# A two-layer diffusion backbone on one core: the second layer's decay masks taken from DRAM, and the sums between the layers put first

## The chip, the cores and the metric

The kernel runs on one core of one Trainium2 chip. The metric is the device time of one execution in microseconds (us). Five engines run their own instruction streams: TensorE (PE in the rows; PEld is its weight load), VectorE (DVE), ScalarE (ACT), GpSimd (POOL) and SyncE (SP), which here only issues DMAs.

## The reference

Two layers over 256 latent and 256 context tokens of width 1024. Each layer mixes tokens by three branches, then runs a mixture of 64 experts:

```
z = h @ w_in[l]                          # split into retention q,k,v,g; attention q,k,v; conv; gates
log_gamma = log_sigmoid(decay_logit)     # (2 directions, 8 heads)
scores = (q @ k^T) * decay_in            # decay_in[i,j] = exp(log_gamma * (i - j)) for i >= j, else 0
y_inner = scores @ v                     # within a chunk of 128 tokens; a state carries to the next chunk
branches = retention, attention (16 heads, 4 kv heads), depthwise conv (width 31) + LayerNorm + silu
mix = (sum_b sigmoid(gate_b) * (branch_b @ w_b)) @ w_out
x = LayerNorm(alpha * x + mod * mix)
f = routed experts (top 8 of 64) + shared expert
x = LayerNorm(alpha * x + mod * f)       # what layer 1 starts from
```

`decay_in` depends on `decay_logit` and positions alone, not on the tokens, so the masks of layer 1 can be worked out at any time after the log of the decay is known.

## The kernel before

**Weights.** fp32 products are made of parts: a weight slab is loaded (tile `raw`, 1 MB per DMA on the SP queue), ScalarE copies it rounded to `whi` (L90), and VectorE or GpSimd subtracts to get the low part `wlo` (L91). `mm` (L228) then does three matmuls per tile (hi·hi, lo·hi, hi·lo). `split_on_pool(n)` gives every n-th piece's low part to GpSimd; 0 means none.

**Start.** Tokens are transposed and modulated into `hb` (hi and lo), the first slab of `w_in` (S_RQ, the retention queries) is split, and TensorE begins with S_RQ. At the same place a series of 25 small VectorE operations (L330 to L352) works out the log of the decays (`lg`, `lgx`) from `decay_logit`.

**Retention** (L606 on). For each of 8 heads `decays` (L613 to L629) builds two mask tiles of 128x512: `ml` (VectorE L618 and L619, GpSimd add L620, ScalarE Exp L621, VectorE adds the identity, L624 twice) and `mx` (ScalarE Exp L626 and L627, GpSimd add L628). The score tile `sa` (L682) is the product of a transposed PSUM tile and `ml`; it is split into `sah` and `sal` for the next matmul. The depthwise convolution (tiles `cacc`, L571, 31 taps by VectorE) has a low priority and fills the stretches where VectorE has nothing else; its `G` (L564) comes from the projections S_CU.

**Merges.** `merge(0)` and `merge(2)` follow: four steps each, in which gate projections give `sg` (ScalarE), an output slab `w_o` is loaded and multiplied, and a part of the modulation matrix (`w_ada`) of later use is worked through. In layer 0 they also end the convolution: the last `cy` goes into `csum` (GpSimd L585), which TensorE multiplies with a mean matrix (L579).

**Between the layers** (L1737 to L1784, written out by hand under `manual_schedule`). Each token tile t of 4 has a base (L1728, L1729) and 8 rows per token from the experts, loaded as four `yb` tiles of 1 MB out of a pool of 7 buffers. `summed(t)` adds rows 0 to 3 on TensorE (identity matmuls L1737, into PSUM) and rows 4 to 7 on VectorE (L1738, L1740), then both (L1743), the gate (L1744) and the residual (L1745), and the statistics. `normal(t)` (L1783, L1784) normalizes `x` on ScalarE; `enter_mix` transposes it (TensorE L382), modulates it and splits it into `hb`. Then layer 1's S_RQ begins. The order of the loop is normal(t), enter_mix(t), summed(t+1).

**Order.** Outside `manual_schedule` a scheduler puts the instructions of each engine in order, by priorities and estimated readiness; the listings below show what it made of each kernel. Tiles of tag `act` (L363, `actt`) share 3 buffers, among them `sg` of the gates and the mask's helper `m`.

Of the kernel before, what the change touches and what calls it, by code (L numbers as in the profile page):

```python
# [21 lines left out]
T = 256  # L22
L = 2
# [46 lines left out]
def body(ctx, tc, A, out):  # L70
# [80 lines left out]
    sp.dma_start(cv, A["cond"].rearrange("p (k n) -> p k n", k=8))  # L151
    FIRST = (0, 4, 1, 5, 2, 6, 3, 7)
# [93 lines left out]
    act.activation(cv, cv, AF.Silu)  # L246
    modrow = dr.tile([L, 6, 2, D], F32, name="modrow")
# [81 lines left out]

    lg = consts.tile([128, L * 16], F32, name="lg")  # L330
    sp.dma_start(lg, A["decay"].to_broadcast([128, L * 16]))
    e_, s_, s2, t_ = (consts.tile([128, L * 16], F32, name=n) for n in ("e_", "s_", "s2", "t_"))
    act.activation(t_, lg, AF.Abs)
    act.activation(e_, t_, AF.Exp, scale=-1.0)
    dve.tensor_scalar(s_, e_, 2.0, None, op0=OP.add)
    dve.reciprocal(s_, s_)
    dve.tensor_tensor(s_, s_, e_, op=OP.mult)
    dve.tensor_tensor(s2, s_, s_, op=OP.mult)
    dve.memset(t_, 1.0 / 19)
    for n in (17, 15, 13, 11, 9, 7, 5, 3, 1):  # L340
        dve.tensor_tensor(t_, t_, s2, op=OP.mult)
        dve.tensor_scalar(t_, t_, 1.0 / n, None, op0=OP.add)
    dve.tensor_tensor(t_, t_, s_, op=OP.mult)
    dve.tensor_scalar(lg, lg, 0.0, None, op0=OP.min)
    dve.scalar_tensor_tensor(lg, t_, -2.0, lg, op0=OP.mult, op1=OP.add)

    lgx = consts.tile([128, 3, L * 8], F32, name="lgx")
    lg4 = lg.rearrange("p (l w h) -> p l w h", l=L, w=2)
    lgo = lgx.rearrange("p i (l h) -> p i l h", l=L)
    dve.tensor_scalar(lgo[:, 0], lg4[:, :, 1], -1.0, None, op0=OP.mult)  # L350
    dve.tensor_scalar(lgo[:, 1], lg4[:, :, 0], 256.0, None, op0=OP.mult)
    dve.tensor_scalar(lgo[:, 2], lg4[:, :, 1], 256.0, None, op0=OP.mult)  # L352

# [6 lines left out]
    x1d = dr.tile([512, D], F32, name="x1d")  # L360

# [13 lines left out]
    def enter(x, w, mod, hi, lo, halves=(0, 1)):  # L375
# [12 lines left out]

    def enter_mix(x, t, mod, halves=(0, 1)):
        ts = slice(t * 128, t * 128 + 128)  # L390
        enter(x, t // 2, mod, hb[:, 0:8, ts], hb[:, 8:16, ts], halves)
# [26 lines left out]
    def mix(l):  # L418
# [30 lines left out]
        with pool_of(f"mix{l}") as M:  # L449
# [18 lines left out]
            def merge(br, bT, between=None):  # L468
# [32 lines left out]
            with pool_of(f"conv{l}") as PC:  # L501
                conv_tile, conv_norm, conv_out = conv(l, PC, NQ, NS, lambda t: projT(wi(S_CU + t), NQ), newT)
                with pool_of(f"ret{l}") as P, split_on_pool(SHARE["ret"][l]):
                    bT = newT()
                    for p in retention(l, P, NQ, NS, NT, lambda s, nt: proj(wi(s), hT, nt),
                                       lambda s: projT(wi(s), NQ), bT):
                        conv_tile(2 * p)
                        conv_tile(2 * p + 1)
                with weight_pool(f"w_merge{l}", *((2, 3), (0, 0))[l]), split_on_pool(3):
                    merge(0, bT, conv_norm)  # L510
                    merge(2, conv_out(newT()))
# [94 lines left out]
    def retention(l, P, NQ, NS, NT, proj_r, proj_t, bT):  # L606
        delta = P.tile([128, 2, T], F32, name="delta")
        sp.dma_start(delta.rearrange("p j i -> p (j i)"), A["delta"])

        def two(name, dt=F32):  # L610
            return P.tile([128, 2, T], dt, name=name, tag=name, bufs=2)

        def decays(head):  # L613

            gf, gb = lg[:, l * 16 + head:l * 16 + head + 1], lg[:, l * 16 + 8 + head:l * 16 + 9 + head]
            ng, f256, b256 = (lgx[:, i, l * 8 + head:l * 8 + head + 1] for i in range(3))
            ml, mx, m2 = two("ml"), two("mx"), actt("m2").rearrange("p (j i) -> p j i", j=2)
            dve.tensor_scalar(ml, delta, 0.0, gf, op0=OP.max, op1=OP.mult)  # L618
            dve.tensor_scalar(m2, delta, 0.0, ng, op0=OP.min, op1=OP.mult)  # L619
            pool.tensor_tensor(ml, ml, m2, op=OP.add)  # L620
            act.activation(ml, ml, AF.Exp)  # L621
            for j in range(2):
                sl = ml[:, j, j * 128:j * 128 + 128]
                dve.tensor_tensor(sl, sl, ident, op=OP.add)  # L624
            m2 = actt("m2").rearrange("p (j i) -> p j i", j=2)
            act.activation(mx, delta, AF.Exp, bias=f256, scale=gf)  # L626
            act.activation(m2, delta, AF.Exp, bias=b256, scale=ng)  # L627
            pool.tensor_tensor(mx, mx, m2, op=OP.add)  # L628
            return ml, mx  # L629

        masks = {0: decays(0)}
        for half in range(2):
# [15 lines left out]
            for pr in range(2):  # L648
# [16 lines left out]
                for hh in range(2):  # L665
                    head = half * 4 + pr * 2 + hh
                    ml, mx = masks.pop(head)
                    if head < 7:
                        masks[head + 1] = decays(head + 1)
# [338 lines left out]
    def moe(l, merged, x_src):  # L1008
# [6 lines left out]
        with pool_of(f"moe{l}") as K, ExitStack() as es:  # L1015
# [698 lines left out]
            with pool_of(f"post{l}") as P:  # L1714
# [16 lines left out]
                def summed(t):  # L1731

                    y = yb[t]
                    o = [bank() for _ in range(2)]
                    for i in range(4):
                        for c in range(2):
                            pe.matmul(o[c], ident, y[i // 2][:, i % 2, c * 512:c * 512 + 512], start=i == 0, stop=i == 3)  # L1737
                    dve.tensor_tensor(y[2], y[2], y[3], op=OP.add)  # L1738
# [17 lines left out]
                with tc.manual_schedule():  # L1756
# [61 lines left out]
    last_modulation()  # L1818
    for k in range(8):
# [101 lines left out]
```

## Time and profile before

| | us |
|---|---|
| median of 3 runs (lowest, highest) | 2847.43 (2845.09, 2849.63) |
| the profiled execution | 2846.9 |
| its span in the trace | 2845.1 |
| TensorE busy | 2573.5 (90%) |
| VectorE, ScalarE, GpSimd busy | 1658.2, 1313.1, 670.9 |

TensorE is the engine that sets the end nearly everywhere: a gain is a stretch in which it now waits and would not. The span splits into the start (to 52 us), layer 0's mixers (to 840), its experts (to 1583), the passage between the layers (to 1690), layer 1's mixers (to 2290) and its experts and end. A row of a timeline gives the start, the busy time, engine, line, operation, out<-in, the count, and in brackets the idle time before it with what released it.

### The profile page before, as it was taken

How to read it: one execution, taken by the hardware profiler on the slowest of the kernel's cores; microseconds unless marked ns; L12 is line 12 of the kernel's file. 1: busy time of each engine (PE TensorE's matmuls, PEld its weight loads, DVE VectorE, ACT ScalarE, POOL GpSimd, SP SyncE). 2: the span in 40 equal slices, each digit the busy share in tenths (PEclk: the TensorE clock that was granted, in tenths of full speed). 3: DMA queues.
4: the chain of work that ended last, by engine and by line, in shares of the span. 5: the costliest groups of instructions: out<-in, count | busy, mean ns of one | idle time of the engine just before them, and what ended most of it. 6: DMA issues, size and time to landing. Idle time of an engine off the chain costs nothing. (4 is left out here: it accounts for less than half of the span.)

```text
span 2845.1 us, 39754 instructions
## 1 busy us (share of the span) xinstructions
PE 2573.5 (90%) x14811; PEld 1865.2 (66%) x14811; DVE 1658.2 (58%) x2967; ACT 1313.1 (46%) x2392; POOL 670.9 (24%) x447
## 2 busy tenths in 40 slices
PE   6999999999987899999999588888989799999995
PEld 4878777788777655555555268877978655554542
DVE  4588795258847555555554577887587722231223
ACT  3443425247742355555555346445477333343431
POOL 2444311222233211122221045532312300000000
PEclk8999999999998899999999798888999799999998
DMA  5212256621152499999999842235415399999996
GB/s 218 75 61 73 85 199 235 223 104 38 64 203 94 192 365 402 405 396 395 399 394 382 347 151 89 90 119 183 174 66 182 122 387 423 421 372 395 417 412 269
DMA packets 118903, 684.13 MB, mean 240 GB/s; under 512 B 21936, under 2 KB 24624, under 8 KB 45744
## 3 DMA queue, kind: packets, MB, share of 16 engines
q1 hardware_dynamic: 92544, 624.80, 56.1%
q0 software_dynamic: 20496, 41.98, 3.9%
q10 hardware_dynamic: 5664, 14.75, 1.3%
q8 instruction: 119, 1.95, 0.3%
q14 instruction: 80, 0.66, 0.1%
HBM read 651.76 MB, written 61.93 MB: 251 GB/s over the span
## 5 line engine op out<-in xcount | busy, mean ns | idle before, releaser
L90 ACT ACTIVATE whi<-raw 128x1024 fp32r<-128x1024 f32 x444 | 457.7, 1053 | 263.4 <-PE mm L228 147.9
L91 POOL TENSOR_TENSOR wlo<-raw,whi 128x1024 fp32r<-128x1024 f32 x140 | 345.7, 2479 | 721.4 <-ACT whi L90 653.8
L91 DVE TENSOR_TENSOR wlo<-raw,whi 128x1024 fp32r<-128x1024 f32 x304 | 374.9, 1254 | 195.9 <-ACT whi L90 191.5
L228 PE MATMUL mm<-whi,hb 128*128 128x256 f32 (+1 forms) x2080 | 423.2, 300 | 29.5 <-ACT whi L90 7.9
L228 PE MATMUL mm<-hb,whi 128*128 128x512 f32 (+1 forms) x1536 | 404.4, 351 | 11.2 <-ACT whi L90 6.2
L228 PEld LDWEIGHTS mm<-whi,hb 128*128 128x128 f32 x2080 | 346.0, 200 | 39.9 <-issue 11.8
L1543 PE MATMUL mm<-raw,xw 128*64 128x512 f32 x1408 | 331.2, 600 | 0.0
L1613 POOL DMA_INDIRECT y<-y,ix x94 | 95.9, 1021 | 976.1 <-ACT y L1609 934.3
L228 PE MATMUL mm<-wlo,hb 128*128 128x256 f32 (+1 forms) x1040 | 310.1, 299 | 12.1 <-POOL wlo L91 8.7
L228 PEld LDWEIGHTS mm<-hb,whi 128*128 128x128 f32 x1536 | 271.2, 196 | 48.2 <-ACT whi L90 6.8
L571 DVE SCALAR_TENSOR_TENSOR cacc<-G,cpk,cacc 128x512 f32<-128x512 f32 (+1 forms) x464 | 287.6, 620 | 10.3
L228 PE MATMUL mm<-hb,wlo 128*128 128x512 f32 (+1 forms) x768 | 269.5, 352 | 4.5 <-POOL wlo L91 3.8
L228 PE MATMUL mm<-whi,xp 128*128 128x512 f32 x736 | 263.3, 411 | 1.7 <-ACT whi L90 1.7
L228 PEld LDWEIGHTS mm<-wlo,hb 128*128 128x128 f32 x1040 | 207.8, 200 | 16.7 <-POOL wlo L91 9.7
L1543 PEld LDWEIGHTS mm<-raw,xw 128*64 128x64 f32 x1408 | 94.6, 136 | 162.4 <-issue 156.7
L228 PE MATMUL mm<-bT,whi 128*128 128x512 f32 (+1 forms) x768 | 193.3, 342 | 0.5 <-ACT sg L459 0.2
L1105 DVE SCALAR_TENSOR_TENSOR hidp<-mm,tab,sgl 128x256 f32<-128x256 f32 x86 | 41.6, 483 | 234.4 <-ACT sgl L1101 233.5
L228 PEld LDWEIGHTS mm<-whi,xp 128*128 128x128 f32 x736 | 139.9, 190 | 50.8 <-ACT whi L90 9.4
L91 DVE TENSOR_TENSOR xp<-tr,xp 128x512 fp32r<-128x512 f32 (+2 forms) x126 | 59.6, 492 | 194.2 <-ACT xp L90 156.2
L1609 ACT ACTIVATE y<-mm 128x512 f32<-128x512 f32 (+1 forms) x188 | 110.1, 594 | 130.2 <-PE mm L1600 69.2
L228 PE MATMUL mm<-wlo,xp 128*128 128x512 f32 x400 | 161.1, 403 | 7.3 <-DVE wlo L91 7.1
L228 PEld LDWEIGHTS mm<-hb,wlo 128*128 128x128 f32 x768 | 150.1, 196 | 25.3 <-POOL wlo L91 4.7
(657 smaller groups left out, 4352.9 us busy)
## 6 DMA issues: line engine op xcount, KB each, us to landing
raw<-in_w_exp SPq DMA_DIRECT2D x384, 1024.0 KB
raw<-in_w_in SPq DMA_DIRECT2D x76, 1024.0 KB
raw<-in_w_ada SPq DMA_DIRECT2D x48, 1024.0 KB
raw<-in_w_o SPq DMA_DIRECT2D x32, 1024.0 KB
yb<-y SPq DMA_DIRECT2D x24, 1024.0 KB
mod<-modrow SPq DMA_DIRECT2D x12, 512.0 KB
raw<-in_w_shared SPq DMA_DIRECT2D x6, 1024.0 KB
x1d<-xr ACTq DMA_DIRECT2D x6, 512.0 KB
```

The source lines that it names most:

```text
L90: act.activation(hi, src, AF.Copy)
L91: eng.tensor_tensor(lo, src, hi, op=OP.subtract)
L228: pe.matmul(o, l_, r_, start=start and i == 0, stop=stop and i == len(ops) - 1)
L571: dve.scalar_tensor_tensor(v(y if j == 30 else acc), G[:, :, j:j + T], cpk[:, t, j:j + 1], v(acc), op0=OP.mult, op1=OP.add)
L1105: dve.scalar_tensor_tensor(o[:n], b[:n, 256:512], gate[:n], sg[:n], op0=OP.mult, op1=OP.mult)
L1543: pe.matmul(os_[s][0][half], xhs[s][0](k)[:, half], raws[index[r, i // 2]][:, k % 4 * 512:k % 4 * 512 + 512], start=k == 0, stop=k == 7)
L1609: act.activation(ys[b][:n, c * 512:c * 512 + 512], o[c], AF.Copy)
L1613: pool.indirect_dma_start(out=y8s[s, b][:], in_=ys[b][:n], in_offset=None, out_offset=bass.IndirectOffsetOnAxis(ap=tabs[s][b][1][:n, 1:2], ...
```

## The change

1. `lg` is loaded second of all and the decay series stands at the head of the program. The first S_RQ slab has its low parts on VectorE.
2. `decays` becomes a function of the whole program. In layer 0's merges `decays_ahead` makes the masks of layer 1's 8 heads, one head at each of the 8 steps, with a priority offset of -100, and stores `ml` and `mx` in DRAM (256 KB each). Layer 1's retention loads them (3 buffers each).
3. Between the layers `summed` is divided into `half` (the TensorE part) and the rest. half(0) and half(1) stand first, half(t+2) behind the entry of tile t; summed(t+1) comes ahead of the low parts of tile t's `hb`, and normal(t+1) behind them. S_RQ's low parts of layer 1 go to GpSimd.

```diff
+    lg = consts.tile([128, L * 16], F32, name="lg")
+    sp.dma_start(lg, A["decay"].to_broadcast([128, L * 16]))
     FIRST = (0, 4, 1, 5, 2, 6, 3, 7)
...
+    def decays_ahead(P, head):
+        ml, mx = (P.tile([128, 2, T], F32, name=n, tag=n, bufs=1) for n in ("ml", "mx"))
+        delta = actt("delta").rearrange("p (j i) -> p j i", j=2)
+        flat = lambda z: z.rearrange("p j i -> p (j i)")
+        sp.dma_start(flat(delta), A["delta"])
+        decays(1, head, delta, ml, mx)
+        for z, m in enumerate((ml, mx)):
+            sp.dma_start(decayed[head, z], flat(m))
...
-            hilo(hi[:, 4 * c:4 * c + 4], lo[:, 4 * c:4 * c + 4], h_.rearrange("p (k n) -> p k n", k=4))
+            if lows is None:
+                hilo(hi_, lo_, h_)
+            else:
+                act.activation(hi_, h_, AF.Copy)
+                lows.append(partial(dve.tensor_tensor, lo_, h_, hi_, op=OP.subtract))
...
+                    if each:
+                        with tc.high_priority(offset=-100):
+                            each(s)
...
-                    merge(0, bT, conv_norm)
-                    merge(2, conv_out(newT()))
+                    ahead = [None, None]
+                    if l == 0:
+                        W = ds_.enter_context(pool_of("decays"))
+                        ahead = [lambda s: decays_ahead(W, s), lambda s: decays_ahead(W, 4 + s)]
+                    merge(0, bT, conv_norm, ahead[0])
+                    merge(2, conv_out(newT()), None, ahead[1])
...
+        def weights_of(head):
+            ml, mx = (two(n, bufs=2 + l) for n in ("ml", "mx"))
+            if l == 0:
+                decays(l, head, delta, ml, mx)
+            else:
+                for z, m in enumerate((ml, mx)):
+                    sp.dma_start(m.rearrange("p j i -> p (j i)"), decayed[head, z])
             return ml, mx
...
-                        ready[l + 1, S_RQ] = [piece(w, j, 4) for j in range(2)]
+                        with split_on_pool(1):
+                            ready[l + 1, S_RQ] = [piece(w, j, 4) for j in range(2)]
+                    half(0)
+                    half(1)
                     summed(0)
...
+                        normal(0)
                         for t in range(NT):
-                            normal(t)
-                            enter_mix(xs[t], t, mod)
+                            lows = []
+                            enter_mix(xs[t], t, mod, lows)
+                            if t + 2 < NT:
+                                half(t + 2)
                             if t + 1 < NT:
                                 summed(t + 1)
+                            for low_ in lows:
+                                low_()
+                            if t + 1 < NT:
+                                normal(t + 1)
...
+    with split_on_pool(0):
+        ready[0, S_RQ] = slab(A["w_in"][S_RQ])
```

VectorE at the start, before; `t__130` is the series, `ml` and `m_409` the first head's masks.

```order
L343 TENSOR_TENSOR t__130<-t__130,s__128 128x32
L345 SCALAR_TENSOR_TENSOR lg<-t__130,lg 128x32
L350 TENSOR_SCALAR lgx<-lg 128x16
L351 TENSOR_SCALAR lgx<-lg 128x16
L352 TENSOR_SCALAR lgx<-lg 128x16
L618 TENSOR_SCALAR ml<-delta,lg 128x512
L619 TENSOR_SCALAR m_409<-delta,lgx 128x512
L618 TENSOR_SCALAR ml<-delta,lg 128x512
L624 TENSOR_TENSOR ml<-ml,cst 128x128 x2
```

VectorE at the same place, after; `h__374` is the last piece of the modulated tokens.

```order
L1880 TENSOR_SCALAR h__368<-xT,modT 128x256 x2
L1880 TENSOR_SCALAR h__374<-xT,modT 128x256 x2
L1881 TENSOR_TENSOR hb<-h__368,hb 128x512
L1881 TENSOR_TENSOR hb<-h__374,hb 128x512
L92 TENSOR_TENSOR wlo<-raw,whi 128x1024 x2
L372 TENSOR_SCALAR ml<-delta,lg 128x512
L373 TENSOR_SCALAR m_420<-delta,lgx 128x512
L372 TENSOR_SCALAR ml<-delta,lg 128x512
```

The series has gone from this place, and the two low parts of S_RQ stand directly behind the last `hb`.

VectorE between the layers, before, from the end of tile 0's sum to the start of tile 1's; `x_15181` is tile 0, `h__15283` and `h__15295` are its two modulated halves, `mm_15306` is TensorE's sum of tile 1.

```order
L1745 TENSOR_TENSOR x_15181<-x_15181,yb 128x1024
L525 BN_STATS bst<-x_15181 128x6 x2
L526 BN_AGGR mv<-bst 128x2
L1783 SCALAR_TENSOR_TENSOR nm<-mv,ny 128x1
L91 TENSOR_TENSOR hb<-h__15283,hb 128x4x128
L91 TENSOR_TENSOR hb<-h__15295,hb 128x4x128
L1738 TENSOR_TENSOR yb<-yb 128x2048
L1740 TENSOR_TENSOR yb<-yb 128x1024
L1743 TENSOR_TENSOR yb<-yb,mm_15306 128x512
```

VectorE at the same place, after; `x_15322` is tile 0, `x_15323` tile 1, `h__15434` and `h__15445` are tile 0's modulated halves.

```order
L570 BN_STATS bst<-x_15322 128x6 x2
L571 BN_AGGR mv<-bst 128x2
L1829 SCALAR_TENSOR_TENSOR nm<-mv,ny 128x1
L1781 TENSOR_TENSOR yb<-yb 128x2048
L1783 TENSOR_TENSOR yb<-yb 128x1024
L1786 TENSOR_TENSOR yb<-yb,mm_15406 128x512
L1786 TENSOR_TENSOR yb<-yb,mm_15407 128x512
L1787 TENSOR_TENSOR yb<-yb,mod_15340 128x1024
L1788 TENSOR_TENSOR x_15323<-x_15323,yb 128x1024
L570 BN_STATS bst<-x_15323 128x6 x2
L571 BN_AGGR mv<-bst 128x2
L1841 TENSOR_TENSOR hb<-h__15434,hb 128x4x128
```

The two low parts of tile 0's `hb` have moved behind the whole of tile 1's sum, which now follows tile 0's `nm` directly. On TensorE, the sum of tile 1 stands ahead of tile 0's transposes and each later sum moves up by one transpose; S_RQ's first matmuls come ahead of tile 2's transposes.

The SP queue in layer 0's merges, before.

```order
L128 DMA raw<-in_w_ada 128x2048 x4
L128 DMA raw<-in_w_o 128x2048
L128 DMA raw<-in_w_in 128x2048
L128 DMA raw<-in_w_ada 128x2048 x4
L128 DMA raw<-in_w_o 128x2048
L128 DMA raw<-in_w_in 128x2048
L128 DMA raw<-in_w_ada 128x2048 x4
L128 DMA raw<-in_w_o 128x2048
```

The SP queue there, after; `decayed` is the DRAM copy of the masks.

```order
L392 DMA decayed<-mx 128x512
L392 DMA decayed<-ml 128x512
L129 DMA raw<-in_w_ada 128x2048
L129 DMA raw<-in_w_in 128x2048
L129 DMA raw<-in_w_ada 128x2048
L389 DMA delta<-in_delta 128x512
L129 DMA raw<-in_w_ada 128x2048 x3
L392 DMA decayed<-ml 128x512
L392 DMA decayed<-mx 128x512
L129 DMA raw<-in_w_o 128x2048
L129 DMA raw<-in_w_ada 128x2048
L129 DMA raw<-in_w_in 128x2048
```

Two stores of a head and one load of `delta` now stand among the weight loads of each step, here one pair directly ahead of a `w_o` load. In layer 1's retention 16 loads of masks stand among the `w_in` loads, and between the layers all 16 `yb` loads now precede the next `w_in` slab, of which one stood ahead of the last `yb` before.

## Rows read from the trace of the kernel before

**Rows 1.** Windows: length, busy PE PEld DVE ACT POOL, clock, DMA share, GB/s

```profile
350.00:600.00 250.00, 249.14 (x1547) 191.51 (x1546) 138.35 (x204) 81.19 (x114) 47.32 (x30) 1.00 0.57 211
1602.00:1617.00 15.00, 6.50 (x14) 2.49 (x12) 14.09 (x15) 0.50 (x2) 0.00 (x0) 0.84 1.02 425
1690.00:1890.00 200.00, 173.50 (x1221) 164.54 (x1221) 159.95 (x293) 110.19 (x153) 106.13 (x63) 0.86 0.26 89
1890.00:1930.00 40.00, 30.85 (x254) 28.05 (x253) 37.10 (x69) 15.68 (x25) 9.66 (x6) 0.87 0.45 166
```

**Rows 2.** Timeline of TensorE at the start: start, busy, work, [idle before <-releaser]

```profile
51.15 0.58 PE L228 MATMUL mm<-wlo,hb 128*128 128x256 f32 x1 [7.18 <-POOL wlo L91]
```

**Rows 3.** Timeline of GpSimd at the start

```profile
38.17 2.88 POOL L91 TENSOR_TENSOR wlo<-raw,whi 128x1024 fp32r<-128x1024 f32 x1 [13.54 <-ACT whi L90]
46.09 1.44 POOL L620 TENSOR_TENSOR ml<-ml,m 128x512 f32<-128x512 f32 x1 [5.04 <-DVE m L619]
...
48.71 4.76 POOL L91 TENSOR_TENSOR wlo<-raw,whi 128x1024 fp32r<-128x1024 f32 x2
```

**Rows 4.** Timeline of VectorE at the start

```profile
38.75 2.35 DVE L341 TENSOR_TENSOR t__130<-t__130,s 128x32 f32<-128x32 f32 x1
```

**Rows 5.** Timeline of TensorE between the layers

```profile
1618.49 1.97 PE L382 MATMUL tr<-cst,x 128*128 128x128 f32 x8 [9.99 <-ACT x L1784]
...
1648.53 0.38 PE L228 MATMUL mm<-whi,hb 128*128 128x256 f32 x1 [1.98 <-DVE yb L1743]
...
1658.85 7.03 PE L1737 MATMUL mm<-yb,cst 128*128 128x512 f32 x16
...
1672.70 0.55 PE L228 MATMUL mm<-whi,hb 128*128 128x256 f32 x1 [3.56 <-DVE yb L1743]
```

**Rows 6.** Timeline of VectorE between the layers

```profile
1605.11 2.35 DVE L91 TENSOR_TENSOR wlo<-raw,whi 128x1024 fp32r<-128x1024 f32 x2
1607.38 2.29 DVE L1738 TENSOR_TENSOR yb<-yb 128x2048 f32<-128x2048 f32 x1
```

**Rows 7.** Timeline of the SP queue between the layers

```profile
1592.10 40.69 SPq L1772 DMA_DIRECT2D yb<-y  x15
```

**Rows 8.** Waits of TensorE, 1690 to 1930 us: total, times, longest

```profile
PE tr L228 <- DVE sa L682: 7.9, 5, 4.6
...
PE mm L228 <- DVE sal L91: 4.4, 2, 3.1
...
PE mm L228 <- DVE G L564: 3.2, 2, 2.6
```

**Rows 9.** Groups on VectorE, 1660 to 1890 us: busy, mean ns, idle before

```profile
L618 DVE TENSOR_SCALAR ml<-delta,lg 128x512 f32<-128x512 f32 x8 | 8.9, 1108 | 0.0
L624 DVE TENSOR_TENSOR ml<-ml,cst 128x128 f32<-128x128 f32 x16 | 8.1, 528 | 3.8 <-ACT ml L621 3.7
...
L619 DVE TENSOR_SCALAR m<-delta,lgx 128x512 f32<-128x512 f32 x8 | 5.7, 714 | 0.0
```

**Rows 10.** Tile ml, 1650 to 1900 us: nanoseconds min/median/max

```profile
L624 DVE TENSOR_TENSOR ml<-ml,cst x16: 277/286/2385, 1689.9 to 1881.1; 128x128 f32<-128x128 f32 x16
L618 DVE TENSOR_SCALAR ml<-delta,lg x8: 475/478/2601, 1686.6 to 1844.3; 128x512 f32<-128x512 f32 x8
```

**Rows 11.** Timeline of all engines, end of layer 0's convolution

```profile
437.74 1.28 POOL L585 TENSOR_TENSOR csum<-csum,cy 128x512 f32<-128x512 f32 x1 [2.39 <-DVE cy L571]
...
442.05 1.02 PE L579 MATMUL aux<-csum,mean_d 128*128 128x512 f32 x2
```

**Rows 12.** Timeline of ScalarE about a table load

```profile
1772.28 0.47 ACT L242 ACTIVATE rs<-aux,eps 128x256 f32<-128x256 f32 x1 [0.79 <-PE aux L692]
1772.78 1.28 ACT L560 ACT_TABLE_LOAD   x1
1774.07 0.38 ACT L560 ACTIVATE sg<-mm 128x256 f32<-128x256 f32 x1
```

**Rows 13.** Timeline of ScalarE in a merge of layer 0

```profile
393.55 2.01 ACT L90 ACTIVATE whi<-raw 128x1024 fp32r<-128x1024 f32 x2 [7.17 <-DMA raw<-in_w_o]
```

More of the change, by code (lines that the diff above doesn't have):

```diff
@@ L1 @@
 import numpy as np
+from functools import partial
 from contextlib import ExitStack, contextmanager
@@ L246, in body @@
     act.activation(cv, cv, AF.Silu)
+    e_, s_, s2, t_ = (consts.tile([128, L * 16], F32, name=n) for n in ("e_", "s_", "s2", "t_"))
+    act.activation(t_, lg, AF.Abs)
+    act.activation(e_, t_, AF.Exp, scale=-1.0)
+    dve.tensor_scalar(s_, e_, 2.0, None, op0=OP.add)
+    dve.reciprocal(s_, s_)
+    dve.tensor_tensor(s_, s_, e_, op=OP.mult)
+    dve.tensor_tensor(s2, s_, s_, op=OP.mult)
+    dve.memset(t_, 1.0 / 19)
+    for n in (17, 15, 13, 11, 9, 7, 5, 3, 1):
+        dve.tensor_tensor(t_, t_, s2, op=OP.mult)
+        dve.tensor_scalar(t_, t_, 1.0 / n, None, op0=OP.add)
+    dve.tensor_tensor(t_, t_, s_, op=OP.mult)
+    dve.tensor_scalar(lg, lg, 0.0, None, op0=OP.min)
+    dve.scalar_tensor_tensor(lg, t_, -2.0, lg, op0=OP.mult, op1=OP.add)
+    lgx = consts.tile([128, 3, L * 8], F32, name="lgx")
+    lg4 = lg.rearrange("p (l w h) -> p l w h", l=L, w=2)
+    lgo = lgx.rearrange("p i (l h) -> p i l h", l=L)
+    dve.tensor_scalar(lgo[:, 0], lg4[:, :, 1], -1.0, None, op0=OP.mult)
+    dve.tensor_scalar(lgo[:, 1], lg4[:, :, 0], 256.0, None, op0=OP.mult)
+    dve.tensor_scalar(lgo[:, 2], lg4[:, :, 1], 256.0, None, op0=OP.mult)
     modrow = dr.tile([L, 6, 2, D], F32, name="modrow")
@@ L327, in mod_b @@
         return t
[L330 to L352, printed above, removed]
     h2d = dr.tile([512, D], F32, name="h2d")
@@ L360, in body, with decays @@
     x1d = dr.tile([512, D], F32, name="x1d")
+    decayed = dr.tile([8, 2, 128, 2 * T], F32, name="decayed")
+    def decays(l, head, delta, ml, mx):
+        gf, gb = lg[:, l * 16 + head:l * 16 + head + 1], lg[:, l * 16 + 8 + head:l * 16 + 9 + head]
+        ng, f256, b256 = (lgx[:, i, l * 8 + head:l * 8 + head + 1] for i in range(3))
+        m2 = actt("m2").rearrange("p (j i) -> p j i", j=2)
+        dve.tensor_scalar(ml, delta, 0.0, gf, op0=OP.max, op1=OP.mult)
+        dve.tensor_scalar(m2, delta, 0.0, ng, op0=OP.min, op1=OP.mult)
+        pool.tensor_tensor(ml, ml, m2, op=OP.add)
+        act.activation(ml, ml, AF.Exp)
+        for j in range(2):
+            sl = ml[:, j, j * 128:j * 128 + 128]
+            dve.tensor_tensor(sl, sl, ident, op=OP.add)
+        m2 = actt("m2").rearrange("p (j i) -> p j i", j=2)
+        act.activation(mx, delta, AF.Exp, bias=f256, scale=gf)
+        act.activation(m2, delta, AF.Exp, bias=b256, scale=ng)
+        pool.tensor_tensor(mx, mx, m2, op=OP.add)
+    def decays_ahead(P, head):
[6 more added lines that the diff above has]
+            sp.dma_start(decayed[head, z], flat(m))
     def actt(name):
@@ L373, in after_norm, with enter @@
         return f[:, 0], f[:, 1]
-    def enter(x, w, mod, hi, lo, halves=(0, 1)):
+    def enter(x, w, mod, hi, lo, halves=(0, 1), lows=None):
         for c in halves:
@@ L386, in enter, with enter_mix @@
                 act.activation(h_[:, ks], p[:, ks], AF.Identity, bias=b, scale=f)
-            hilo(hi[:, 4 * c:4 * c + 4], lo[:, 4 * c:4 * c + 4], h_.rearrange("p (k n) -> p k n", k=4))
-    def enter_mix(x, t, mod, halves=(0, 1)):
+            hi_, lo_, h_ = hi[:, 4 * c:4 * c + 4], lo[:, 4 * c:4 * c + 4], h_.rearrange("p (k n) -> p k n", k=4)
+            if lows is None:
[3 more added lines that the diff above has]
+                lows.append(partial(dve.tensor_tensor, lo_, h_, hi_, op=OP.subtract))
+    def enter_mix(x, t, mod, lows):
         ts = slice(t * 128, t * 128 + 128)
-        enter(x, t // 2, mod, hb[:, 0:8, ts], hb[:, 8:16, ts], halves)
+        enter(x, t // 2, mod, hb[:, 0:8, ts], hb[:, 8:16, ts], lows=lows)
     def row(name):
@@ L466, in keep_gate, with merge @@
                 sp.dma_start(gd[s, :, :NQ], sg)
-            def merge(br, bT, between=None):
+            def merge(br, bT, between=None, each=None):
                 for s in range(4):
+                    if each:
+                        with tc.high_priority(offset=-100):
+                            each(s)
                     if between and s == 3:
@@ L508, in mix @@
                         conv_tile(2 * p + 1)
-                with weight_pool(f"w_merge{l}", *((2, 3), (0, 0))[l]), split_on_pool(3):
-                    merge(0, bT, conv_norm)
-                    merge(2, conv_out(newT()))
+                with weight_pool(f"w_merge{l}", *((2, 3), (0, 0))[l]), split_on_pool(3), ExitStack() as ds_:
+                    ahead = [None, None]
[4 more added lines that the diff above has]
+                    merge(2, conv_out(newT()), None, ahead[1])
             open_aux(2)
@@ L606, in retention, with two @@
     def retention(l, P, NQ, NS, NT, proj_r, proj_t, bT):
[L607 to L628, printed above, removed]
+        def two(name, dt=F32, bufs=2):
+            return P.tile([128, 2, T], dt, name=name, tag=name, bufs=bufs)
+        if l == 0:
+            delta = two("delta", bufs=1)
+            sp.dma_start(delta.rearrange("p j i -> p (j i)"), A["delta"])
+        def weights_of(head):
+            ml, mx = (two(n, bufs=2 + l) for n in ("ml", "mx"))
+            if l == 0:
+                decays(l, head, delta, ml, mx)
+            else:
+                for z, m in enumerate((ml, mx)):
+                    sp.dma_start(m.rearrange("p j i -> p (j i)"), decayed[head, z])
             return ml, mx
-        masks = {0: decays(0)}
+        masks = {0: weights_of(0)}
         for half in range(2):
@@ L668, in retention @@
                     if head < 7:
-                        masks[head + 1] = decays(head + 1)
+                        masks[head + 1] = weights_of(head + 1)
                     o = 64 * hh
@@ L1729, in base, with half @@
                     dve.scalar_tensor_tensor(xs[t], xs[t], ALPHA, f, op0=OP.mult, op1=OP.add)
-                def summed(t):
+                sums = {}
+                def half(t):
                     y = yb[t]
-                    o = [bank() for _ in range(2)]
+                    o = sums[t] = [bank() for _ in range(2)]
                     for i in range(4):
@@ L1737, in summed @@
                             pe.matmul(o[c], ident, y[i // 2][:, i % 2, c * 512:c * 512 + 512], start=i == 0, stop=i == 3)
+                def summed(t):
+                    y, o = yb[t], sums.pop(t)
                     dve.tensor_tensor(y[2], y[2], y[3], op=OP.add)
```

## The prediction

> **What bounds the kernel now.** I read the windows by stage first, to find where TensorE waits, then its waits in those stages, then the timelines around them. Layer 0's merges have no room: TensorE is busy 249.14 of 250 us there. Layer 1's retention has some: 173.50 of 200 us at a granted clock of 0.86, with VectorE busy 159.95, and the stretch behind it has 30.85 of 40 with VectorE at 37.10 [rows 1]. The start has one wait of 7.18 us for GpSimd's low part [rows 2]. Between the layers TensorE waits for `x`, which comes out of VectorE's chain (9.99 us for the first tile), and for the PSUM banks that VectorE frees late [rows 5]. So the change touches three places where TensorE waits and one where it does not.
>
> **A, the start.** GpSimd makes S_RQ's first low part at 38.17 in 2.88 us, then takes up the first head's mask add, which waits 5.04 us for VectorE's `m`; only at 48.71 do the next low parts start [rows 3]. VectorE's `m` is late because of the series of 25 small operations, one of which took 2.35 us beside GpSimd [rows 4]. After the change the series is done while tokens are still loaded, and the two low parts stand on VectorE directly behind `hb`; a pair takes 2.35 us there [rows 6]. The second is then ready near 41.5, before TensorE has finished the first (43.97, which is 51.15 less 7.18) [rows 2]. The wait of 7.2 goes, and the first low part comes about 0.8 us sooner than 38.17 + 2.88 = 41.05. The load of `lg` costs one issue ahead of the `w_ada` loads. I take **-8**, between -6.5 (the low parts stretched by GpSimd's next one, as the 0.2 us operation was) and -8.7. What is late next at the start is S_RK's low part behind the same mask add, but TensorE has the second half of S_RQ to do first.
>
> [...]
>
> **B, layer 1's retention.** Gone from VectorE: 8.9 + 8.1 + 5.7 = 22.7 us [rows 9], from 32 instructions whose undisturbed durations are 0.48 and 0.28 us and whose longest are 2.6 and 2.4 [rows 10]; GpSimd's 16 adds and ScalarE's 24 exponentials go too. Of TensorE's waits those for `sa` (7.9 us) and `sal` (4.4) follow from `ml` or from a VectorE stretched beside GpSimd, 12.3 in all; of the 3.2 for `G` I count half, since the convolution's filling work then ends sooner [rows 8]. That is **-14**. The lower bound on the gain is half of `sa`'s wait, -4, if what follows it is late in its own right; the upper is nearly all of the stretch's idle 26.5 us [rows 1], -24. Added are 16 loads of 256 KB: 4.2 MB at the 425 GB/s seen between the layers is 10 us over a stretch whose DMA share is 0.26 [rows 1], with three buffers for each mask, so they lie beside other work. They stand in SP's queue ahead of `w_in` loads; a load that waits for its buffer holds those back, and the `whi` copies after them. That price I bound by the same -4.
>
> **C, layer 0's merges.** The 22.7 us come back here as 8 heads, but beside a TensorE that is full. What can end later is the convolution. VectorE's new order has the masks of nearly four heads ahead of the last `cy`: 3.75 heads at 2 x 0.48 + 2 x 0.28 = 1.5 us, 5.7 us, and with some stretching [rows 10] about 7.5. GpSimd's `csum` ends at 437.74 + 1.28 = 439.02 and TensorE takes it at 442.05 [rows 11], so 3.0 of it is hidden: **+4.5**. The matmuls queued behind that one (a gate projection) wait with it. From the second merge on VectorE has room. At best 0, if the scheduler's place for the matmul leaves it room; at worst +16: the ScalarE order has 13 more table loads in these merges (7 fewer in layer 1's retention), 13 x 1.28 [rows 12] = 16.6 us, all of it in the way of `sg`.
>
> In this trace the activation ahead of a table load ends right before it and the next one starts right behind its 1.28 us [rows 12]. The Trainium skill ("ScalarE: Activation LUTs", What ACT_TABLE_LOAD costs) gives 1283 ns and a drain of about 1380 ns more, 2.66 us for a switch. By it the worst case would be an estimated 35 us instead of 16.6; no drain is seen in these rows, so it adds nothing to the sum.
>
> **D, between the layers.** Two low parts leave VectorE's chain, 2.35 us ahead of tile 0's first sum [rows 6]; GpSimd has nothing there. In before a tile takes 1618.49 - 1607.38 = 11.1 us from VectorE's first add to TensorE's transposes [rows 5, 6]. Sixteen loads of 1.05 MB from 1592.10 [rows 7] at 425 GB/s [rows 1] end at 1631.6 if buffers never hold them; the 14th, the last that TensorE's sum of tile 3 needs, lands near 1627. In the new order that sum stands ahead of S_RQ. With its 7.03 us [rows 5], a little more at a lower clock, behind tile 1's transposes it ends near 1638, and S_RQ starts there instead of at 1648.53: -10.5. The 7.03 us no longer stand in the middle of S_RQ, and the wait of 3.56 behind them goes: -10.6 more, -21.1 together. Against that stands the entry of tile 3: 1631.6 + 11.1 = 1642.7 for its transposes, and some 4 us for modulation and parts, 1647; S_RQ's first half with tile 2's transposes, 10.3 us as from 1648.53 to 1658.85 [rows 5], is done at 1648.3. That is level, and any slip shows; I allow 3 us for it: **-18**, between -11 (only the earlier start) and -23. One `w_in` load that stood ahead of the last `yb` now stands behind it, but the `yb` stream ends some 11 us sooner.
>
> **E, the last passage.** VectorE's and TensorE's orders are as before there: 0.
>
> **The sum**: -8 - 14 + 4.5 - 18 = -35.5. The profiled execution took 2846.9, which gives 2811.4; the median of the runs shown is 0.5 above it, so I forecast **2812**.
>
> **Rivals.**
> 1. The retention's gain is given back by the convolution. For it: VectorE is busy 37.1 of 40 us behind the retention, TensorE waits there too [rows 1], so VectorE may be the bound with its taps. Against it: those 22.7 us leave just this engine. B is then -3: 2823.
> 2. The merges pay fully, C at +16: 2823 or 2824. For it, TensorE has no idle time there; against it, the gate matmuls and the `w_ada` work lie between `sg` and its use.
> 3. All waits go: B -24, C 0, D -23, A -8: -55, 2792. For it: the clock of 0.86 rises when TensorE waits less. Against it: other waits follow.
> 4. Slower. In SP's order the two stores of a head stand directly ahead of a `w_o` load in the merges. A store waits for GpSimd's add, which waits for the exponentials and for one of three shared buffers that the gates' `sg` also use. The `w_o` load comes just in time already: ScalarE waits 7.17 us for one [rows 13]. The gains of A, B and D are 40 us; this decides from a delay of (40 + 6) / 8 = 5.8 us at each of 8 steps, and at 6.5 us, 52 in all, gives 2859.
> 5. The change does not do what it says: layer 1's mask loads come late and TensorE waits for them as it did for `sa`, and TensorE's sums between the layers wait for buffers as long as before. A alone less C remains: -8 + 4.5, 2844.
>
> **How the numbers follow.** Forecast 0.50, rival 1 0.20, rival 2 0.12, rival 3 0.10, rival 4 0.04, rival 5 0.04. No change means within 0.2%, 5.7 us, what a measurement of this kernel can tell. Faster: 0.50 + 0.20 + 0.12 + 0.10 = 0.92; same 0.04 (rival 5); slower 0.04. The range: 2796, half-way into rival 3, to 2833, past rivals 1 and 2 together with a D of -11. The forecast's own range is 2804 to 2821.
>
> **What would show it.** A: no wait for a GpSimd low part near 44, S_RQ's second low part used at about 43. B: `sa` and `sal` no longer among TensorE's longer waits, no `L618`-like rows in layer 1. C: a wait of TensorE for `csum` of about 4 us near 435, and otherwise a full window. D: S_RQ starting some 46 us after the first `yb` issue instead of 56, with loads running without a gap. Wrong is the forecast if TensorE waits for `w_o` in every merge step, if layer 1's retention keeps some 20 idle us per 200, or if tile 3's entry leaves a wait of 10 us or more.

## The result, and the profile after

The changed kernel takes 2796.09 us in the median (2792.94 to 2800.77), the kernel before beside it 2846.38: a ratio of 0.9823 (95% interval 0.9806 to 0.984), 50 us faster. Forecast were 2812 us, with 2804 to 2821 as the forecast's own range and 2796 to 2833 with its rivals: the direction is right, but the time lies below the first range and on the very edge of the second, and the gain is 1.4 times what was forecast. The profiled execution took 2795.08, its span is 2792.9.

The same instructions in both traces (TensorE's order is nearly the same) give marks, and the time between two marks is what a stretch cost. A lead, below, is by how much a matmul comes sooner than the same one of the other kernel. In us:

| from, to | before | after | difference | forecast |
|---|---|---|---|---|
| start, sum of the convolution (L579, L624) | 442.1 | 434.8 | -7.2 | A -8, C +4.5 |
| that sum, first sum of expert rows (`mm<-yb`) | 1157.1 | 1157.6 | +0.5 | |
| that, first transposes of S_RQ's result (`tr<-cst,z`) | 87.0 | 65.2 | -21.8 | D -18 |
| those, first matmul of layer 1's merge (`mm<-bT`) | 217.6 | 186.4 | -31.2 | B -14 |
| that, transposes of `xr` at layer 1's experts | 314.7 | 321.6 | +6.9 | 0 |
| those, first sum of the last passage (`mm<-yb`) | 591.7 | 592.2 | +0.5 | 0 |

The sum is -52.3, the difference of the spans. The retention alone is 17 us over its forecast, as much as the whole excess (52 for 35.5); the first two rows together are 3 over, the passage 4, and a row that was not in the forecast takes 7 back.

**The start.** TensorE of the changed kernel (the row's columns are as in [rows 2]) uses the first low part at 40.05, and no wait is left until 44 us:

```profile
40.05 0.58 PE L231 MATMUL mm<-wlo,hb 128*128 128x256 f32 x1 [0.46 <-DVE wlo L92]
```

VectorE makes both low parts in 2.36 us behind `hb`; the first mask operation behind them takes 2.61 us beside GpSimd instead of 0.48:

```profile
38.76 2.36 DVE L92 TENSOR_TENSOR wlo<-raw,whi 128x1024 fp32r<-128x1024 f32 x2 [0.26 <-ACT whi L91]
41.04 2.61 DVE L372 TENSOR_SCALAR ml<-delta,lg 128x512 f32<-128x512 f32 x1
```

The matmul that stood at 51.15 [rows 2] now stands at 42.77: -8.4, where -8 was forecast.

**Layer 0's merges.** From the matmuls at 379 us to those at 588 the lead over before falls from 9.4 to 6.0, so the merges cost 3.4. TensorE's waits in the stretch from 350 to 600 us (total, times, longest), in before:

```profile
PE mm L228 <- POOL wlo L91: 0.9, 1, 0.9
```

and after:

```profile
PE mm L231 <- POOL wlo L92: 1.7, 1, 1.7
PE aux L624 <- POOL csum L630: 1.5, 1, 1.5
PE mm L321 <- DVE G L609: 1.1, 1, 1.1
PE mm L231 <- DVE wlo L92: 0.7, 1, 0.7
```

TensorE waits 1.5 for `csum`, not 4.5. The low part of GpSimd's that it waited for in before as well now stands behind a mask add and costs 0.8 more, and a low part of VectorE's costs 0.7 (the wait for `G` comes ahead of the matmuls at 379). ScalarE's new table loads are there, 21 in this stretch against 7 (two of the groups, busy time and mean ns), and none of the waits above is for `sg`:

```profile
L497 ACT ACT_TABLE_LOAD x8 | 10.3, 1283 | 0.8 <-issue 0.6
...
L380 ACT ACT_TABLE_LOAD x7 | 9.0, 1283 | 14.4 <-issue 9.5 <-DMA delta<-in_delta 4.9
```

**Between the layers.** The 16 `yb` loads are issued without a long gap (before: 15 in 40.69 us and the last 10 us later [rows 7]):

```profile
1585.47 32.60 SPq L1815 DMA_DIRECT2D yb<-y  x16
```

TensorE's sums follow each other, and the wait for `x` is 1.48 and 1.95 where it was 9.99 for the first tile [rows 5]:

```profile
1592.44 17.04 PE L1776 MATMUL mm<-yb,cst 128*128 128x512 f32 x32 [16.53 <-DMA yb<-y]
1610.96 1.09 PE L415 MATMUL tr<-cst,x 128*128 128x128 f32 x8 [1.48 <-ACT x L1830]
...
1621.37 1.34 PE L415 MATMUL tr<-cst,x 128*128 128x128 f32 x8 [1.95 <-ACT x L1830]
...
1630.46 0.68 PE L231 MATMUL mm<-whi,hb 128*128 128x256 f32 x1
```

S_RQ starts 45.0 us after the first issue (1630.46 - 1585.47); it was 56.4.

**Layer 1's retention.** The windows of the changed kernel (columns as in [rows 1]): the merges, 15 us between the layers, and the retention between its marks:

```profile
350.00:600.00 250.00, 244.94 (x1553) 188.82 (x1551) 149.99 (x232) 115.50 (x152) 66.06 (x45) 1.00 0.61 223
1605.00:1620.00 15.00, 12.68 (x35) 5.53 (x33) 13.87 (x19) 6.40 (x15) 0.00 (x0) 1.00 1.01 421
1657.70:1844.00 186.30, 178.29 (x1378) 169.34 (x1377) 159.77 (x286) 97.83 (x140) 89.31 (x49) 0.97 0.34 119
```

The retention between the same marks in the kernel before:

```profile
1686.20:1903.80 217.60, 190.41 (x1357) 180.92 (x1356) 176.51 (x323) 122.15 (x170) 111.66 (x65) 0.87 0.25 88
```

TensorE's idle time falls from 27.2 (217.60 - 190.41) to 8.0 us, which is 19.2 of the 31.2. The other 12.1 are busy time: the matmuls take 178.29 instead of 190.41, at a mean granted clock of 0.97 instead of 0.87 (a mean of stretches at 2.4 GHz and stretches at 1.2). What a level costs can be read from two pieces of the retention in before, the first at 1.2 GHz and the second at 2.4:

```profile
1706.00:1716.00 10.00, 8.83 (x34) 7.79 (x34) 4.66 (x7) 5.84 (x9) 5.51 (x3) 0.50 0.13 25
1716.00:1764.00 48.00, 43.87 (x350) 42.11 (x349) 38.16 (x73) 33.24 (x47) 28.25 (x16) 1.00 0.30 106
```

That is 0.26 us of busy time a matmul against 0.13. By the means, some 55 of 217.6 us were at the lower level in before and some 11 of 186.3 after, in one piece near the end:

```profile
1660.00:1816.00 156.00, 148.07 (x1175) 140.91 (x1174) 135.09 (x241) 84.08 (x117) 83.71 (x44) 1.00 0.36 125
1817.00:1826.00 9.00, 9.00 (x36) 7.68 (x36) 6.49 (x13) 3.26 (x6) 2.36 (x1) 0.50 0.33 117
```

What TensorE waited for in the retention of before, beside `sa` (7.9), `sal` (4.4) and `G` (3.2) of [rows 8]:

```profile
PE tr L643 <- DVE z L412: 3.4, 2, 2.1
PE mm L228 <- ACT sah L90: 2.7, 1, 2.7
PE mm L228 <- ACT rg L663: 2.5, 1, 2.5
PE mm L228 <- ACT sg L560: 2.3, 1, 2.3
```

What it waits for there now:

```profile
PE mm L231 <- DVE sal L92: 4.5, 5, 2.2
PE mm L231 <- ACT sah L91: 1.0, 1, 1.0
PE mm L231 <- ACT sg L605: 0.8, 1, 0.8
PE tr L231 <- DVE sa L719: 0.7, 1, 0.7
PE tr L680 <- DVE z L450: 0.5, 1, 0.5
PE mm L231 <- DVE G L609: 0.2, 1, 0.2
```

`sa` is all but gone, and so are `G`, `z` and `rg`; `sal`, which was to go with `sa`, is as long as before.

### The profile page after: what moved, and what is told of

Read it like the earlier page. It is cut to its first block, busy times and chain, and to the rows that moved or that the text cites. A ratio compares the mean times of both kernels' runs of the same rounds, so it can differ in the third digit from the quotient of the medians.

```text
span 2792.9 us, 39847 instructions
## 1 busy us (share of the span) xinstructions
PE 2554.4 (91%) x14811; PEld 1848.9 (66%) x14811; DVE 1658.7 (59%) x2967; ACT 1322.5 (47%) x2398; POOL 669.7 (24%) x447
## 3 DMA queue, kind: packets, MB, share of 16 engines
q8 instruction: 119, 1.95, 0.3%
## 5 line engine op out<-in xcount | busy, mean ns | idle before, releaser
L231 PE MATMUL mm<-hb,whi 128*128 128x512 f32 (+1 forms) x1536 | 397.1, 346 | 6.5 <-ACT whi L91 4.7
```

The costliest lines, as they stand in the source:

```text
L231: pe.matmul(o, l_, r_, start=start and i == 0, stop=stop and i == len(ops) - 1)
```

## The experiments

Each ratio is to the kernel before run beside it; differences to the changed kernel are differences of these ratios, times 2846 us.

**Each part alone.** The kernel before with one part of the diff each (no further edit), and the changed kernel without mask work in the merges.

> The kernel before with the start alone changed: log of the decays loaded second, series first, low parts of the first S_RQ slab on VectorE. Theory (each stretch's gain belongs to the edit made there): 8 to 10 us faster than before, all of it by 55 us of the span. Rival (the start's gain is partly lost again because later stretches are bound by loads that do not start sooner): 0 to 5 us faster, with the lead shrinking in layer 0's retention or merges.

Measured: 0.9955 (0.9939 to 0.9972), 13 us faster. The second low part is used at 42.70; the lead is 8.5 us there and 8 to 14 at the later marks to 2280 us, with no trend.

> The kernel before with the passage between the layers alone changed. Theory: 19 to 23 us faster, S_RQ about 11 us after the new order allows, and layer 1's retention as long as before (214 us between its first mark and the first retention product of the merge). Rival (the passage also speeds the retention behind it, because loads of w_in start sooner and TensorE comes in at a higher clock): 30 us faster or more, with the retention some 10 to 15 us shorter though its masks are still worked out there.

Measured: 0.994 (0.9919 to 0.9961), 17 us faster; in the profiled execution the passage is 20.7 us shorter (66.3 for 87.0), and the retention is not shorter but 4.6 longer (222.2).

> The kernel before with the masks of layer 1 worked out ahead and loaded, start and passage as before. Theory: retention of layer 1 shorter by 27 to 31 us, merges of layer 0 longer by 3 to 4, and about 22 to 27 us faster in all. Rival (half of the retention's gain came with the new passage): retention 12 to 16 us shorter, 9 to 13 us faster in all.

Measured: 0.992 (0.9904 to 0.9937), 23 us faster. The retention takes 190.5, 27 less, with the old passage in front of it; behind it 9 us are lost (324.1 for 314.7). The three parts alone make 13 + 17 + 23 = 53 us, the whole 50: they add up within the intervals. The rival that the passage speeds the retention by 10 to 15 us falls; 4 us at most may be its part (190.5 here, 186.4 with all parts together).

```
-                    if l == 0:
+                    if l > 9:
                         W = ds_.enter_context(pool_of("decays"))
...
-                    sp.dma_start(m.rearrange("p j i -> p (j i)"), decayed[head, z])
+                    sp.dma_start(m.rearrange("p j i -> p (j i)"), A["delta"])
```

> The changed kernel with no mask work in layer 0's merges; layer 1 loads the table of distances in place of its masks, same sizes and same number of loads, so its retention's values differ from the reference. Theory (the mask work in the merges costs TensorE 3 to 4 us, by the convolution's sum and a late low part): 3 to 4 us faster than the changed kernel. Rival (the merges' mask work costs nothing in the end, since TensorE's loss there is made up by a later wait for loads): within 1 us of the changed kernel.

Measured: 0.9805 (0.9784 to 0.9827), 5 us under the changed kernel's ratio with overlapping intervals. In the trace the lead over the changed kernel is 3 to 7 us between the merges and layer 1, and of the waits in the merges a single one of 0.9 is left, as before. But the lead is 3.2 at 1850 us and gone at 2280, and the two profiled spans differ by 1.0 (2791.9 and 2792.9). So a price of about 4 is seen at the merges; that it lasts to the end is not shown, and the rival is not excluded.

**What made layer 1's masks dear.** These kernels put mask work back into layer 1's retention, with results that nobody reads: first all of it.

```
-        if l == 0:
-            delta = two("delta", bufs=1)
...
+        delta = two("delta", bufs=1)
...
                     sp.dma_start(m.rearrange("p j i -> p (j i)"), decayed[head, z])
+                decays(l, head, delta, two("mu"), two("mv"))
```

> The changed kernel, in which layer 1's retention loads its masks and also works them out as the kernel before did, into tiles that nobody reads. Theory 1 (the gain there is engine time: VectorE, GpSimd and ScalarE stretched each other and TensorE's clock fell with its waits): 20 to 30 us slower than the changed kernel, the retention (182 us there) at 200 us or more. Theory 2 (the gain is the wait for ml in the chain from scores to sa): within 6 us of the changed kernel.

Measured: 0.9953 (0.9935 to 0.9971), 37 us slower than the changed kernel. Windows of the retention, 229.4 us long (43 longer than in the changed kernel and 12 longer than in the one before, which has no mask loads there), and TensorE's wait for `sa`:

```profile
1659.90:1889.30 229.40, 198.30 (x1381) 187.80 (x1380) 181.99 (x327) 122.75 (x171) 112.94 (x65) 0.86 0.28 95
```

```profile
PE tr L231 <- DVE sa L719: 7.7, 5, 4.6
```

No one reads `ml` here, and TensorE waits 7.7 us for `sa` all the same: it was not `ml`'s chain that held `sa` up, but the engines and buffers it shares with the masks. Theory 2 falls.

```
# dve_masks, per head              # pool_masks, per head           # act_masks, per head
dve.tensor_scalar x2 (128x512)     pool.tensor_tensor x2 (128x512)  act.activation Exp x3 (128x512)
dve.tensor_tensor x2 (128x128)
```

> The changed kernel with only VectorE's four operations per head of the mask work kept in layer 1's retention, unread. If VectorE's own time is the cost: 10 to 20 us slower than the changed kernel, for 12 us of undisturbed work (8 heads at 1.5 us) with the convolution's tail moved by as much. If the cost is the collision with GpSimd's adds or the wait for ml: under 5 us slower.

> The changed kernel with two GpSimd adds per head in layer 1's retention, unread. If the cost is GpSimd holding up VectorE's two-input operations and its own low parts: 8 to 20 us slower than the changed kernel for 16 x 1.3 = 21 us of GpSimd. If it is VectorE's own time: under 4 us slower.

> The changed kernel with only ScalarE's three exponentials per head kept in layer 1's retention, unread: 18 us of ScalarE, which is busy for some 95 of 182 us there. If ScalarE's own time or its table loads are the rest of the masks' price (37 us in all, of which VectorE's operations gave 11 to 13 and GpSimd's 7): 10 to 20 us slower than the changed kernel. If the rest comes from the engines' holding each other up: under 5 us slower.

Measured: 0.9868 (0.9844 to 0.9892), 0.9847 (0.9821 to 0.9873) and 0.9842 (0.9819 to 0.9865), or 13, 7 and 5 us slower than the changed kernel; the retention took 198.5, 193.6 and 191.2 for 186.4. Together 24 of 43 us in the retention. VectorE's share is the size of its undisturbed time, 12 us; GpSimd's and ScalarE's lie between the two answers given, and neither is the main thing.

The rest was sought in the three buffers of tag `act`: the helper `m` shares them with `sa` and `vc`, so that these may have to wait until ScalarE and GpSimd have done with `m`.

```
-        m2 = actt("m2").rearrange("p (j i) -> p j i", j=2)
+        m2 = own("mh") if own else actt("m2").rearrange("p (j i) -> p j i", j=2)
...
+                decays(l, head, delta, two("mu"), two("mv"), two)
```

> As the run with layer 1's masks worked out unread, but the helper m in two buffers of its own instead of the three that it shared with sa, vc and sg. If the shared buffers made the masks dear (sa and vc wait until a mask's m is free): 12 us or more faster than that run, at about 2820 us. If engine time alone did: within 5 us of it, 2829 to 2838.

Measured: 0.9909 (0.9886 to 0.9932), 12 us faster than with shared buffers, the low end of what the theory gave. The retention is 211.2 long, 18 less, and the wait for `sa` falls:

```profile
1655.90:1867.10 211.20, 192.76 (x1379) 183.38 (x1378) 187.52 (x314) 114.20 (x165) 111.65 (x65) 0.89 0.31 106
```

```profile
PE tr L231 <- DVE sa L719: 2.4, 3, 1.0
```

12 + 7 + 5 for the engines and 18 for the buffers are 42 of the 43 us. The same edit was then made in the kernel before, where the masks are read:

> The kernel before, with one thing changed: in layer 1's retention the masks' helper m has two buffers of its own and no longer shares three with sa, vc and sg. If a good part of the retention's gain was those buffers coming free and not mask work leaving: 10 to 16 us faster than before, with the retention about 200 us long (218 before, 186 after the change). If engine time was all of it: within 4 us of before.

Measured: 0.998 (0.997 to 0.9989), 6 us faster, between the two answers. The retention is 205.0 us long, 13 shorter, but the stretch behind it 325.2 for 314.7:

```profile
1685.30:1890.30 205.00, 183.49 (x1357) 175.06 (x1355) 187.40 (x315) 113.14 (x164) 114.32 (x65) 0.92 0.27 94
```

So buffers coming free are some 13 of the retention's 31 us, and no mask work has to leave for them; they are worth 6 in the end, since the stretch behind gives most of the rest back.

**The merges and the give-back.** All 8 heads in the second merge:

```
-                        ahead = [lambda s: decays_ahead(W, s), lambda s: decays_ahead(W, 4 + s)]
+                        ahead = [None, lambda s: [decays_ahead(W, 2 * s + i) for i in range(2)]]
```

> The changed kernel with all 8 heads' masks in the second merge of layer 0, two a step, none in the first. Theory (the merges' price of 3 to 5 us is the convolution's sum, which ends in the first merge): 2 to 4 us faster than the changed kernel, no wait for csum. Rival (two heads a step crowd ScalarE and the three shared buffers): 0 to 10 us slower, with waits for sg in the second merge.

Measured: 0.981 (0.979 to 0.983), 4 us under the changed kernel's ratio, inside its interval. The wait for `csum` is gone, with 3.0 us of slack as before (timeline of all engines):

```profile
424.79 1.29 POOL L630 TENSOR_TENSOR csum<-csum,cy 128x512 f32<-128x512 f32 x1 [2.40 <-DVE cy L616]
...
429.11 1.02 PE L624 MATMUL aux<-csum,mean_d 128*128 128x512 f32 x2
```

Behind the retention the changed kernel loses 6.9 us. The largest piece stands where layer 1's first normalized rows `xr` are transposed: TensorE waits there (total, times, longest)

```profile
PE tr L415 <- DVE xr L580: 11.2, 2, 6.2
```

which was 5.4 before. VectorE works out a root in operations on one column. After:

```profile
2159.20 0.16 DVE L592 SCALAR_TENSOR_TENSOR ny<-na,ny 128x1 f32<-128x1 f32 x1
2159.40 2.39 DVE L591 SCALAR_TENSOR_TENSOR na<-ny,nv 128x1 f32<-128x1 f32 x1
2161.83 2.26 DVE L592 SCALAR_TENSOR_TENSOR ny<-na,ny 128x1 f32<-128x1 f32 x1
2164.12 0.22 DVE L591 SCALAR_TENSOR_TENSOR na<-ny,nv 128x1 f32<-128x1 f32 x1
```

and GpSimd at that time

```profile
2159.43 4.64 POOL L92 TENSOR_TENSOR wlo<-raw,whi 128x1024 fp32r<-128x1024 f32 x2 [0.28 <-DVE ny L592]
```

The kernel before, VectorE and GpSimd:

```profile
2216.36 0.16 DVE L547 SCALAR_TENSOR_TENSOR ny<-na,ny 128x1 f32<-128x1 f32 x1
2216.55 0.22 DVE L546 SCALAR_TENSOR_TENSOR na<-ny,nv 128x1 f32<-128x1 f32 x1
2216.81 0.16 DVE L547 SCALAR_TENSOR_TENSOR ny<-na,ny 128x1 f32<-128x1 f32 x1
2217.01 0.22 DVE L546 SCALAR_TENSOR_TENSOR na<-ny,nv 128x1 f32<-128x1 f32 x1
```

```profile
2217.84 6.19 POOL L91 TENSOR_TENSOR wlo<-raw,whi 128x1024 fp32r<-128x1024 f32 x2 [1.53 <-ACT whi L90]
```

Two operations of 0.2 us take 2.39 and 2.26, as long as GpSimd's two subtractions last, 4.3 us lost at this place. In the kernel before the subtractions began 0.4 us after the root's last such operation. Not all of the 4.3 stays lost: before, TensorE had one more wait right behind these transposes, for their split `hb`, which it no longer has:

```profile
PE aux L1059 <- DVE hb L91: 4.5, 1, 4.5
```

The lead, 57.2 us ahead of the transposes and 52.9 behind them, is back at 54.8 there, and falls to 53.0 over the second tile's entry. Two kernels move GpSimd's work away from there.

```
# behind: the parts are issued on ScalarE behind the first tile's modulation
+                            es_.enter_context(tc.issue_after(entered[0].ins))
                             steps.extend(dense(A["w_shared"][l], ...))
# shared_dve: in layer 1 their low parts are VectorE's
-                    with split_on_pool(1):
+                    with split_on_pool(1 - l):
                         steps.extend(dense(A["w_shared"][l], ...))
```

> The changed kernel with the parts of layer 1's shared expert issued on ScalarE behind the first tile's modulation, so that GpSimd makes no low parts while VectorE works out the first tile's root. Theory (the changed kernel loses 4 us there because two of VectorE's 0.2 us operations take 2.3 us beside GpSimd): the first transposes of xr wait 2 us instead of 6, 3 to 4 us faster. Rival (the low parts then come late for the shared expert, or hold up the second tile's root): 0 to 6 us slower.

> The changed kernel with the low parts of layer 1's shared expert on VectorE instead of GpSimd; two of them stand within the first tile's root there. Theory (GpSimd's collisions cost 4.3 us at that place): the root's small operations take 0.2 us again, but 2.4 us of low parts take their place: 1 to 3 us faster. Rival (VectorE is the bound there): 0 to 5 us slower.

Measured: `behind` 0.983 (0.9813 to 0.9846), no gain: the stretch up to `xr` is 317.7 for 321.6, 3.9 shorter as the theory has it, and the experts behind it 599.7 for 592.2, which is the rival's part. `shared_dve` 0.9792 (0.9771 to 0.9813), 9 us under the changed kernel's ratio. Its wait for `xr` is gone, but others stand in its place:

```profile
PE aux L1096 <- DVE hb L92: 4.0, 1, 4.0
PE aux L1095 <- ACT hb L91: 3.9, 2, 2.1
...
PE tr L415 <- DVE xr L580: 1.7, 2, 1.2
```

That is 7.9 us of other waits, and its span is only 3.2 us shorter than the changed kernel's, so the 9 are not explained. Both edits together, and the changed kernel again beside them:

> The changed kernel with the masks of all 8 heads in the second merge and the low parts of layer 1's shared expert on VectorE. If the two gains seen alone (3.7 and some 3 to 8 us) add up: 5 to 12 us faster than the changed kernel. If they were differences between chips or runs: within 3 us of it.

> The changed kernel once more, on the chip of the runs beside it: 2790 to 2800 us, 48 to 54 us faster than before; its retention within 3 us of 186 and the stretch from there to layer 1's expert entry at 318 to 324, if the 7 us lost there (315 before) belong to the kernel and not to one run.

Measured: 0.9807 (0.9791 to 0.9824) and 0.982 (0.9804 to 0.9836), medians of 2791.29 and 2793.75. The two edits together cannot be told from none: the gains seen singly don't add up. The repeat has the same retention (184.3), the same loss behind it (323.8) and the same two stretched operations (2.36 and 2.26), so these belong to the kernel.

## Why the prediction was right in direction and short in size

- **A, -8: right.** -8.4 in the trace, by the way described; what kept the second low part late was its place behind the mask adds on GpSimd.
- **C, +4.5: near in size, half right in place.** 3.4 by the lead over before, 4.6 by that of `c_free` at the end of the merges. `csum` came 5.1 us late against TensorE's work, not 7.5 (its end moved by 4.3, from 439.02 to 434.77, TensorE's work ahead of it by 9.4); 3.0 of that were hidden, as the text has it. One low part of GpSimd's and one of VectorE's gave the rest. The upper bound of 16, all 14 new table loads in the way of `sg`, was far off: TensorE has no wait for `sg` there.
- **D, -18: short by 4.** S_RQ started where the text put it (45.0 us after the first `yb` issue, 46 forecast). Of the 3 us allowed for tile 3's entry none was needed; a wait for GpSimd at 1649.81 took 3.8 instead, and a little more than the -21.1 of the text's first sum came in.
- **B, -14: the step that failed.** The retention became 31.2 us shorter. The text had the right stretch, but sized the term by three waits: `sa` and `sal` whole and half of `G`. `sa` and `G` went, 10.2 together; `sal` did not (4.5 for 4.4). The waits for `z`, `sah`, `rg`, `sg` and `sq`, which the text put at nothing without a reason, gave 9.1 more. Most of these waits come with the mask work even where nobody reads it: in `idle_masks` they are 4.8 for `z`, 3.2 for `rg`, 2.3 for `sg` and 7.7 for `sa`, and the retention is 43 us longer, 24 of them through the engines and 18 through the shared buffers. And 12.1 us came from TensorE's busy time, which the text had noted as a clock of 0.86 and given no price in B; its upper bound of 24, taken from the idle time, was no bound where the clock is below full. Rival 3 named that clock as the reason for a larger gain and got 0.10.
- **Behind the retention, 0: wrong.** 6.9 us are given back up to `xr`, 4.3 of them in one collision of VectorE with GpSimd, of which 1.9 return for a while right behind. Rival 1 had looked for a give-back in the convolution's tail; there the lead shrinks by 2 to 3 us (from 59.8 at the first `mm<-bT` to 57.1 at 2057).
- **E and rivals 2, 4 and 5.** The last passage is unchanged (35.1 us for 34.9). No step of the merges waits for `w_o` on TensorE; mask stores and loads land 2.0 to 7.5 us after their issue (13 of 32, those whose landing the trace shows), and no wait of TensorE names them.

Open is the rest of what the stretch behind the retention loses. It takes 321.6 to 325.6 us in the eight profiled executions with the collision, and 314.7 to 317.7 in six of the nine without it; but 321.7 in `idle_own`, which has none, and 321.8 and 324.7 where VectorE makes those low parts. From the merge's first matmul to the end of the span it is 947.6 to 953.8 with the collision, 941.3 to 946.6 in the six without it that leave the shared expert's low parts alone, and 946.3 to 951.9 in the three that move them. So the collision goes with the loss, but taking it away does not bring all of it back: that it is the cause is not shown, and what takes its place in the last three was not tried. Why the subtractions come earlier against the root after the change is open too: in both kernels ScalarE's copies ahead of them follow the landing of the shared expert's weights, but no run varied that. Nor did a run change the clock without the waits: how the two hang together is read from the rows alone.

## What to carry to other kernels

Work off the critical path still has a price through the buffers it shares: before moving it, give its helper tiles buffers of their own and measure. Where TensorE's mean granted clock is below full, price a removed wait at more than its length: here 19 us of waits brought 31. When a stretch is rid of work, list all of its waits, not only those whose releaser is that work. And after a change that shifts engines against each other by a few us, look again at chains of very small VectorE operations: here they were where GpSimd hit.

## What the runs showed of the hardware

An operation of 0.16 to 0.22 us on one column of VectorE took 2.3 us beside a GpSimd subtraction of 128x1024, in every kernel where the two met (2.39 and 2.26; 2.36 and 2.26 in the repeat; 2.21 to 2.38 in six others). In the retention the mean granted clock was 0.86 to 0.87 with 27 to 31 idle us, 0.89 with 18, 0.92 with 22, and 0.97 with 8, so it did not follow the idle total alone. At 1.2 GHz a matmul of the retention took 0.26 us of busy time on the mean, and at 2.4 GHz 0.13. An operation of VectorE with a single tile as input, the mask's TENSOR_SCALAR of 128x512, took 2.61 us beside GpSimd's subtraction instead of 0.48.
